# A batched matmul on one Trainium2 core: x loaded eight matrices at a time into single buffers

## The chip, the cores and the metric

The kernel runs on one core of one Trainium2 chip. The metric is the device time in microseconds, the median of several executions. "Span" is the time from the first to the last instruction in one profiled execution; it is some 1.5 to 1.8 us below the time. All runs that are compared here are of the fast state, but for three runs of a single execution, whose state is unknown; they are marked.

## The reference

```python
b1, b2, m, k, n = 8, 16, 256, 512, 384
x      = randn(b1, b2, m, k)   # float32
weight = randn(b1, b2, k, n)   # float32
return np.matmul(x, weight)    # float32
```

These are 128 products of 256x512 by 512x384. 167.8 MB are read, 50.3 MB are written.

## The kernel before

A round takes four matrices. Each partition gets 16 KB of x (eight rows), 12 KB of weights per pair of matrices, and gives back 12 KB of output. ScalarE casts x to bf16, and TensorE transposes pairs of bf16 as if they were fp32 words. VectorE copies the transposes out of PSUM and casts the weights, TensorE multiplies, ScalarE copies the result out, and SyncE issues all transfers on one queue. x has two landing buffers:

```python
XS, WS, OS = 2, 2 * G // D, 4        # landing slots of x, weights, output
BS, TS, WBS = 1, 2, 2 * G            # x in bf16, transposed x, weights in bf16
...
def load(e, t, U, s):
    n = t * U + s
    if not isinstance(n, int) or n >= XS:
        e.wait_ge(x_cast, n + (1 - XS))          # the cast of two rounds before
    e.dma_start(x_sb[s % XS][:], ...)            # 2 MB, runs of 16 KB
    for d in range(G // D):
        ...
        e.dma_start(w_sb[slot][:], ...)          # 1.5 MB
...
def step(t, U, s, more):                         # ScalarE
    for q in range(T):
        copy_out(e, t, U, s, q)
        if q == 1 and more:
            cast_x(e, t, U, s + 1)               # next round's x, amid the copies out
```

## Time and profile before

| | before |
|---|---|
| time, median | 519.8 us (519.78 to 519.87) |
| span | 518.3 us |
| transfers | 218.16 MB, 131 of them on one queue |
| busy share of PE, VectorE, ScalarE | 61%, 62%, 41% |

The page's slices cut the span in 40 equal parts; a digit is the busy share in tenths, and the row GB/s is what the sixteen DMA engines moved. The groups and the timeline give an instruction's line, its engine, what it writes and reads, and in brackets how long the engine was idle before it and what ended that. The lines are shown in the prediction below. The issuing engine's own waits, in total us, number and longest, show how tightly the queue was fed:

```profile
SPq L100 <- ACT x_bf L130: 257.1, 30, 9.4
SPq L108 <- DVE w_bf L148: 138.1, 58, 3.6
```

SyncE waits 257 us for x casts, yet a transfer takes a median of some 26 us from issue to landing. So these waits lie beside a long queue and cost nothing.

### The profile page before, as it was taken

To read this page: it belongs to the slowest core of one execution; us is meant where nothing else is said; L and a number is where in the kernel's file an instruction comes from. 1 tells how busy PE (TensorE), PEld (TensorE's weight loads), DVE (VectorE), ACT (ScalarE), POOL (GpSimd) and SP (SyncE) were. 2 spreads that over 40 slices of the span, in tenths; PEclk is the share of its full clock that TensorE was granted. 3 is DMA by queue.
4 is the path that set the end of the run, shared out by engine and by line. 5 is a ranking of instruction groups with operands and counts; after the bars stand their busy time and mean duration, and the time that the engine had idled before them with its cause. 6 is when DMAs were issued, how large, how long until landed. Compare 5 with 4: busy or idle time off the path is not lost.

```text
span 518.3 us, 11239 instructions
## 1 busy us (share of the span) xinstructions
PE 315.5 (61%) x4608; PEld 198.8 (38%) x4608; DVE 323.9 (62%) x384; ACT 212.7 (41%) x193; POOL 0.7 (0%) x6
## 2 busy tenths in 40 slices
PE   0686773576655675655756557665567665675653
PEld 0455452343433443433424334343344333443331
DVE  0878867655577555775556765557755577555670
ACT  3065462454234553245542445423454324553242
POOL 0000000000000000000000000000000000000000
PEclk9988788877687778678776877778787868886787
DMA  8999999999999999999999999999999999999995
GB/s 332 431 426 426 427 427 429 430 426 429 430 428 429 431 426 428 428 431 431 425 429 429 430 430 429 427 428 429 430 430 428 426 431 430 429 428 427 428 431 214
DMA packets 18868, 218.16 MB, mean 421 GB/s; under 512 B 2096, under 2 KB 2096, under 8 KB 2608
## 3 DMA queue, kind: packets, MB, share of 16 engines
q1 hardware_dynamic: 18864, 218.11, 99.2%
q8 instruction: 2, 0.03, 0.0%
q14 instruction: 2, 0.02, 0.0%
HBM read 167.77 MB, written 50.33 MB: 421 GB/s over the span
## 4 chain that ended last, share of the span: by engine, by line
DMA 81%; DVE 12%; issue 2%; PE 2%; ACT 1%; SPq 0%; DVEq 0%; ACTq 0%
DMA w_sb<-in_weight_dram 81%; DVE w_bf L148 12%; PE po L181 2%; ACT x_bf L130 0%; DVEq _compat.py:109 0%; SPq L108 0%; ACT out_sb L195 0%; SPq L100 0%; DVE x_t L154 0%; DVEq L143 0%; DVEq L230 0%; SPq L107 0%; ACTq L194 0%; SPq L288 0%; SPq L54 0%
## 5 line engine op out<-in xcount | busy, mean ns | idle before, releaser
L148 DVE CAST w_bf<-w_sb 64x1536 bf16<-64x1536 f32 x256 | 244.5, 955 | 179.4 <-DMA w_sb<-in_weight_dram 166.7
L181 PE MATMUL po<-w_bf,x_t 128*32 128x384 bf16 x4096 | 231.4, 400 | 121.0 <-DVE x_t L154 121.0
L195 ACT COPY out_sb<-po 128x768 f32<-128x768 f32 x128 | 99.2, 802 | 290.2 <-PE po L181 290.2
L181 PEld LDWEIGHTS po<-w_bf,x_t 128*32 128x32 bf16 x4096 | 124.5, 117 | 225.4 <-DVE x_t L154 130.9
L167 PE MATMUL pt<-identity,x_bf 128*128 128x128 f32 x512 | 84.0, 329 | 73.0 <-ACT x_bf L130 73.0
L130 ACT CAST x_bf<-x_sb 128x2048 bf16<-128x2048 f32 x64 | 118.4, 1901 | 6.1 <-DMA x_sb<-in_x_dram 6.1
L167 PEld LDWEIGHTS pt<-identity,x_bf 128*128 128x128 f32 x512 | 74.3, 213 | 84.9 <-issue 84.9
L154 DVE COPY x_t<-pt 128x1024 bf16<-128x1024 bf16 x128 | 79.5, 683 | 1.0
L130 ACT ACT_TABLE_LOAD x1 | 1.3, 1283 | 1.3 <-PEq L237 1.3
masks.py:199 POOL TENSOR_SCALAR_AFFINE_SELECT identity<-identity 128x128 f32<-128x128 f32 x1 | 0.3, 292 | 0.2 <-POOL identity L204 0.2
L204 POOL MEMSET identity<- 128x128 f32 x1 | 0.2, 204 | 0.5 <-SPq L54 0.5
L277 POOL MEMSET const-bfloat16-1.0<- 128x1 bf16 x1 | 0.1, 101 | 0.0
L277 POOL MEMSET const-uint8-127<- 128x1 uint8 x1 | 0.1, 101 | 0.0
L277 POOL MEMSET const-float32-0.0<- 128x1 f32 x1 | 0.1, 98 | 0.2 <-issue 0.2
L277 POOL MEMSET const-float32-1.0<- 128x1 f32 x1 | 0.1, 98 | 0.0
## 6 DMA issues: line engine op xcount, KB each, us to landing
w_sb<-in_weight_dram SPq DMA_DIRECT2D x64, 1536.0 KB, 27.5
x_sb<-in_x_dram SPq DMA_DIRECT2D x32, 2048.0 KB, 25.8
out_dram<-out_sb SPq DMA_DIRECT2D x31, 1536.0 KB, 30.6
out_dram<-out_sb SPq DMA_DIRECT2D x4, 384.0 KB, 3.6
```

The costliest lines, as they stand in the source:

```text
L130: ins = e.copy(out=x_bf[s % BS][:, :, h], in_=x_sb[s % XS][:].rearrange("p r (q s c) -> p r s q c", s=S, c=KO)[:, :, h],)
L148: e.tensor_copy(out=w_bf[(s * G + d * D + a) % WBS][h * HP : (h + 1) * HP], in_=w_sb[slot][a * HP : (a + 1) * HP, h * KO : (h + 1) * KO, : ...
L154: e.tensor_copy(out=x_t[s % TS][:, 2 * q : 2 * q + 2], in_=pt[(s * T + q) % PT][:].bitcast(bf16),).then_inc(t_copied, 1)
L167: ins = e.transpose(pt[(s * T + q) % PT][:, rr, h, :], words[:, 2 * q + rr, h :: KO // 2], identity[:],)
L181: ins = e.matmul(po[(s * T + q) % PO][mine, rr, :N], x_t[s % TS][:, 2 * q + rr, ko // 2, mine, ko % 2], w_bf[(s * G + i) % WBS][:, ko, :], ...
L195: e.copy(out=out_sb[s % OS][:, 2 * q : 2 * q + 2, :], in_=po[(s * T + q) % PO][:, :, :N],).then_inc(o_copied, 1)
L204: e.memset(identity[:], 0.0).then_inc(id_done, 1)
L277: nc = _bacc.Bacc("TRN2", target_bir_lowering=False, num_devices=1)
```

## The change

A group is now eight matrices. One x load brings 4 MB in runs of 32 KB into the only x buffer, and x_bf and x_t have one slot each as well. Transposes of the two halves of rows are written alternately into PSUM, word by word, so that 32 columns of x_t are one slice. Leaving out the drains on GpSimd is a side matter. The core of the diff:

```diff
-    XS, WS, OS = 2, 2 * G // D, 4
-    BS, TS, WBS = 1, 2, 2 * G
+    WS, OS, WBS = GX // D, 4, GX           # GX = 8
...
-    x_sb = sbuf("x_sb", [P, R, K], fp32, XS)
+    x_sb = sbuf("x_sb", [P, F * R, K], fp32)[0]      # F = 2
...
+    def load_x(e, n):
+        if not isinstance(n, int) or n > 0:
+            e.wait_ge(x_cast, n * (F * S))           # all four casts of the group before
+        e.dma_start(
+            x_sb[:], x_rows[bass.ds(n * (GX * M), GX * M)].rearrange("(p r) k -> p r k", p=P)
+        ).then_inc(x_in, 16)
...
                     ins = e.transpose(
-                        pt[(s * T + q) % PT][:, rr, h, :],
-                        words[:, 2 * q + rr, h :: KO // 2],
+                        pt[r % PT][:, h, :, f],
+                        words[:, f * R + r, h :: KO // 2],
...
     @block.scalar
-        cast_x(e, 0, NG, 0)
-        with e.Fori(0, NG // U - 1) as t:
-            for s in range(U):
-                step(t, U, s, True)
...
+        with e.Fori(0, NX // U) as t:
             for s in range(U):
-                step(t, U, s, True)
+                cast_x(e, t * U + s)
+                for f in range(F):
+                    copy_out(e, t * U + s, f, s * F + f, t)
```

More of the change, by code (lines that the diff above doesn't have):

```diff
@@ L39 @@
     G = 4
+    F = 2
+    GX = F * G
     C = P // G
@@ L45, with sbuf @@
     HP = P // D
-    NG = B // G
-    XS, WS, OS = 2, 2 * G // D, 4
-    BS, TS, WBS = 1, 2, 2 * G
+    NX = B // GX
+    WS, OS, WBS = GX // D, 4, GX
     PT, PO = 4, 2
     LAG = 4
-    ctx.enter_context(tc.tile_critical())
-    def sbuf(name, shape, dtype, n):
+    ctx.enter_context(tc.tile_critical(no_gpsimd_drain=True))
+    def sbuf(name, shape, dtype, n=1):
         return [
@@ L67, in sems @@
         return [tc.alloc_semaphore(f"{name}{s}") for s in range(n)]
-    identity = sbuf("identity", [P, P], fp32, 1)[0]
-    x_sb = sbuf("x_sb", [P, R, K], fp32, XS)
-    x_bf = sbuf("x_bf", [P, R, S, HP, KO], bf16, BS)
-    x_t = sbuf("x_t", [P, R, KO // 2, P, 2], bf16, TS)
+    identity = sbuf("identity", [P, P], fp32)[0]
+    x_sb = sbuf("x_sb", [P, F * R, K], fp32)[0]
+    x_bf = sbuf("x_bf", [P, F * R, S, HP, KO], bf16)[0]
+    x_t = sbuf("x_t", [P, R, KO // 2, P, F, 2], bf16)[0]
     w_sb = sbuf("w_sb", [P, S * KO, N], fp32, WS)
@@ L77 @@
     out_sb = sbuf("out_sb", [P, R, N], fp32, OS)
-    pt = psum("pt", [P, 2, KO // 2, P], fp32, PT)
+    pt = psum("pt", [P, KO // 2, P, F], fp32, PT)
     po = psum("po", [P, 2, 512], fp32, PO)
-    id_done, x_cast, w_cast, t_made, t_copied, p_made, o_copied = (
+    id_done, x_cast, w_cast, t_made, t_copied, p_made, o_copied, x_in = (
         sems(name, 1)[0]
         for name in (
-            "id_done", "x_cast", "w_cast", "t_made", "t_copied", "p_made", "o_copied"
+            "id_done", "x_cast", "w_cast", "t_made", "t_copied", "p_made", "o_copied",
+            "x_in",
@@ L88 @@
         )
     )
-    x_in, w_in, o_out = sems("x_in", XS), sems("w_in", WS), sems("o_out", OS)
+    w_in, o_out = sems("w_in", WS), sems("o_out", OS)
     BIAS = 8
-    def load(e, t, U, s):
-        n = t * U + s
-        if not isinstance(n, int) or n >= XS:
-            e.wait_ge(x_cast, n + (1 - XS))
+    def load_x(e, n):
+        if not isinstance(n, int) or n > 0:
+            e.wait_ge(x_cast, n * (F * S))
         e.dma_start(
-            x_sb[s % XS][:],
-            x_rows[bass.ds(n * (G * M), G * M)].rearrange("(p r) k -> p r k", r=R),
-        ).then_inc(x_in[s % XS], 16)
-        for d in range(G // D):
-            slot = (s * (G // D) + d) % WS
-            if not isinstance(n, int) or n >= 2:
-                e.wait_ge(w_cast, n * (G * S) + ((d + 1) * D * S - 2 * G * S))
+            x_sb[:], x_rows[bass.ds(n * (GX * M), GX * M)].rearrange("(p r) k -> p r k", p=P)
+        ).then_inc(x_in, 16)
@@ L108, in load, with load_w @@
+    def load_w(e, n, f):
+        for d in range(f * G // D, (f + 1) * G // D):
+            if not isinstance(n, int) or n > 0:
+                e.wait_ge(w_cast, n * (GX * S) + ((d + 1) * D * S - GX * S))
             e.dma_start(
-                w_sb[slot][:],
-                w_rows[bass.ds(n * (G * K) + d * (D * K), D * K)].rearrange(
-                    "(p k) n -> p k n", k=S * KO
-                ),
-            ).then_inc(w_in[slot], 16)
-    def store(e, t, U, s, pieces=1):
-        n = t * U + s
-        dram = o_rows[bass.ds(n * (G * M), G * M)].rearrange("(p r) n -> p r n", r=R)
+                w_sb[d][:],
+                w_rows[bass.ds(n * (GX * K) + d * (D * K), D * K)].rearrange(
+                    "(p k) n -> p k n", p=P
+                ),
+            ).then_inc(w_in[d], 16)
@@ L118, in store @@
+    def store(e, n, f, slot, pieces=1):
+        dram = o_rows[bass.ds(n * (GX * M) + f * (G * M), G * M)].rearrange(
+            "(p r) n -> p r n", p=P
+        )
         for q in range(pieces):
             rows = slice(q * R // pieces, (q + 1) * R // pieces)
-            e.wait_ge(o_copied, n * T + ((q + 1) * T // pieces + BIAS))
-            e.dma_start(out=dram[:, rows], in_=out_sb[s % OS][:, rows]).then_inc(
-                o_out[s % OS], 16
-            )
-    def cast_x(e, t, U, s):
-        n = t * U + s
-        e.wait_ge(x_in[s % XS], (t * (U // XS) + s // XS) * 16 + 16)
-        e.wait_ge(t_made, n * T + ((1 - BS) * T + BIAS))
-        for h in range(S):
-            ins = e.copy(
-                out=x_bf[s % BS][:, :, h],
-                in_=x_sb[s % XS][:].rearrange("p r (q s c) -> p r s q c", s=S, c=KO)[
-                    :, :, h
-                ],
-            )
-        ins.then_inc(x_cast, 1)
@@ L138, in prepare @@
-    def prepare(e, t, U, s):
-        n = t * U + s
-        e.wait_ge(p_made, n * T + (BIAS - T))
-        for d in range(G // D):
-            slot = (s * (G // D) + d) % WS
-            e.wait_ge(
-                w_in[slot], (t * (U * G // D // WS) + s * G // D // WS) * 16 + 16
-            )
-            for a in range(D):
-                for h in range(S):
-                    e.tensor_copy(
-                        out=w_bf[(s * G + d * D + a) % WBS][h * HP : (h + 1) * HP],
-                        in_=w_sb[slot][a * HP : (a + 1) * HP, h * KO : (h + 1) * KO, :],
-                    ).then_inc(w_cast, 1)
-        for q in range(T):
-            e.wait_ge(t_made, n * T + (q + 1 + BIAS))
-            e.tensor_copy(
-                out=x_t[s % TS][:, 2 * q : 2 * q + 2],
-                in_=pt[(s * T + q) % PT][:].bitcast(bf16),
-            ).then_inc(t_copied, 1)
@@ L159, in multiply @@
-    def multiply(e, t, U, s):
-        n = t * U + s
-        words = x_bf[s % BS][:].rearrange("p r s q c -> p r (s q c)").bitcast(fp32)
-        e.wait_ge(x_cast, n + 1)
-        for q in range(T):
-            e.wait_ge(t_copied, n * T + (q + 1 - PT + BIAS))
-            for rr in range(2):
+            e.wait_ge(o_copied, n * (F * T) + (f * T + (q + 1) * T // pieces + BIAS))
+            e.dma_start(out=dram[:, rows], in_=out_sb[slot][:, rows]).then_inc(
+                o_out[slot], 16
+            )
@@ new lines, in cast_x, with cast_w @@
+    def cast_x(e, n):
+        e.wait_ge(x_in, n * 16 + 16)
+        e.wait_ge(t_made, n * R + BIAS)
+        for f in range(F):
+            rows = slice(f * R, (f + 1) * R)
+            for s in range(S):
+                e.copy(
+                    out=x_bf[:, rows, s],
+                    in_=x_sb[:, rows].rearrange("p r (q s c) -> p r s q c", s=S, c=KO)[
+                        :, :, s
+                    ],
+                ).then_inc(x_cast, 1)
+    def cast_w(e, n, f):
+        e.wait_ge(p_made, n * (F * T) + (f * T + T - F * T + BIAS))
+        for d in range(f * G // D, (f + 1) * G // D):
+            e.wait_ge(w_in[d], n * 16 + 16)
+            for a in range(D):
+                for s in range(S):
+                    e.tensor_copy(
+                        out=w_bf[d * D + a][s * HP : (s + 1) * HP],
+                        in_=w_sb[d][a * HP : (a + 1) * HP, s * KO : (s + 1) * KO, :],
+                    ).then_inc(w_cast, 1)
@@ new lines, in copy_xt, with transpose @@
+    def copy_xt(e, n):
+        e.wait_ge(p_made, n * (F * T) + BIAS)
+        for r in range(R):
+            e.wait_ge(t_made, n * R + (r + 1 + BIAS))
+            e.tensor_copy(out=x_t[:, r], in_=pt[r % PT][:].bitcast(bf16)).then_inc(
+                t_copied, 1
+            )
+    def transpose(e, n):
+        words = x_bf[:].rearrange("p r s q c -> p r (s q c)").bitcast(fp32)
+        e.wait_ge(x_cast, n * (F * S) + F * S)
+        for r in range(R):
+            e.wait_ge(t_copied, n * R + (r + 1 - PT + BIAS))
+            for f in range(F):
@@ L172, in multiply @@
             ins.then_inc(t_made, 1)
-        e.wait_ge(w_cast, n * (G * S) + G * S)
+    def multiply(e, n, f):
+        e.wait_ge(w_cast, n * (GX * S) + (f + 1) * G * S)
         for q in range(T):
-            e.wait_ge(t_copied, n * T + (q + 1 + BIAS))
-            e.wait_ge(o_copied, n * T + (q + 1 - PO + BIAS))
+            if f == 0:
+                e.wait_ge(t_copied, n * R + (2 * q + 2 + BIAS))
+            e.wait_ge(o_copied, n * (F * T) + (f * T + q + 1 - PO + BIAS))
             for rr in range(2):
@@ L179, in multiply @@
                     for i in range(G):
-                        mine = slice(i * C, (i + 1) * C)
+                        lanes = slice((f * G + i) * (P // GX), (f * G + i + 1) * (P // GX))
                         ins = e.matmul(
-                            po[(s * T + q) % PO][mine, rr, :N],
-                            x_t[s % TS][:, 2 * q + rr, ko // 2, mine, ko % 2],
-                            w_bf[(s * G + i) % WBS][:, ko, :],
+                            po[q % PO][i * C : (i + 1) * C, rr, :N],
+                            x_t[:, 2 * q + rr, ko // 2, lanes, :, ko % 2].rearrange(
+                                "k p f -> k (p f)"
+                            ),
+                            w_bf[f * G + i][:, ko, :],
                             start=(ko == 0),
@@ L188, in multiply, with copy_out @@
             ins.then_inc(p_made, 1)
-    def copy_out(e, t, U, s, q):
-        n = t * U + s
-        if q == 0:
-            e.wait_ge(o_out[s % OS], (t * (U // OS) + s // OS) * 16 + 16)
-        e.wait_ge(p_made, n * T + (q + 1 + BIAS))
-        e.copy(
-            out=out_sb[s % OS][:, 2 * q : 2 * q + 2, :],
-            in_=po[(s * T + q) % PO][:, :, :N],
-        ).then_inc(o_copied, 1)
-    block = ctx.enter_context(nc.Block())
+    def copy_out(e, n, f, slot, turn):
+        e.wait_ge(o_out[slot], turn * 16 + 16)
+        for q in range(T):
+            e.wait_ge(p_made, n * (F * T) + (f * T + q + 1 + BIAS))
+            e.copy(
+                out=out_sb[slot][:, 2 * q : 2 * q + 2, :], in_=po[q % PO][:, :, :N]
+            ).then_inc(o_copied, 1)
+    block = ctx.enter_context(nc.Block(no_gpsimd_drain=True))
     @block.gpsimd
@@ L207, in _ @@
         e.drain().then_inc(id_done, 1)
+    U = OS // F
+    BACK = LAG // F
     @block.sync
     def _(e):
-        U = OS
-        for n in range(LAG):
-            load(e, 0, NG, n)
-        rounds = (NG - LAG) // U
+        for n in range(BACK):
+            load_x(e, n)
+            for f in range(F):
+                load_w(e, n, f)
+        rounds = (NX - BACK) // U
         with e.Fori(0, rounds) as t:
             for s in range(U):
-                load(e, t, U, LAG + s)
-                store(e, t, U, s)
-        for n in range(rounds * U, NG):
-            if n + LAG < NG:
-                load(e, 0, NG, n + LAG)
-            store(e, 0, NG, n, T if n == NG - 1 else 1)
+                load_x(e, t * U + (BACK + s))
+                for f in range(F):
+                    load_w(e, t * U + (BACK + s), f)
+                    store(e, t * U + s, f, (s * F + f) % OS)
+        for n in range(rounds * U, NX):
+            if n + BACK < NX:
+                load_x(e, n + BACK)
+            for f in range(F):
+                if n + BACK < NX:
+                    load_w(e, n + BACK, f)
+                last = n == NX - 1 and f == F - 1
+                store(e, n, f, (n * F + f) % OS, T if last else 1)
         for s in range(OS):
-            e.wait_ge(o_out[s], 16 + 16 * (NG // OS + (T - 1 if s == (NG - 1) % OS else 0)))
+            e.wait_ge(o_out[s], 16 + 16 * (NX // U + (T - 1 if s == OS - 1 else 0)))
     @block.vector
     def _(e):
-        U = 2
         e.sem_inc(t_copied, BIAS)
-        with e.Fori(0, NG // U) as t:
-            for s in range(U):
-                prepare(e, t, U, s)
+        with e.Fori(0, NX) as n:
+            cast_w(e, n, 0)
+            copy_xt(e, n)
+            for f in range(1, F):
+                cast_w(e, n, f)
     @block.tensor
     def _(e):
-        U = 2
         e.sem_inc(t_made, BIAS)
@@ L239, in _ @@
         e.wait_ge(id_done, 2)
-        with e.Fori(0, NG // U) as t:
-            for s in range(U):
-                multiply(e, t, U, s)
+        with e.Fori(0, NX) as n:
+            transpose(e, n)
+            for f in range(F):
+                multiply(e, n, f)
     @block.scalar
     def _(e):
-        U = OS
         e.sem_inc(o_copied, BIAS)
@@ L249, in _ @@
             e.sem_inc(o_out[s], 16)
-        def step(t, U, s, more):
-            for q in range(T):
-                copy_out(e, t, U, s, q)
-                if q == 1 and more:
-                    cast_x(e, t, U, s + 1)
-        cast_x(e, 0, NG, 0)
-        with e.Fori(0, NG // U - 1) as t:
+        with e.Fori(0, NX // U) as t:
             for s in range(U):
-                step(t, U, s, True)
-        for n in range(NG - U, NG):
-            step(0, NG, n, n < NG - 1)
+                cast_x(e, t * U + s)
+                for f in range(F):
+                    copy_out(e, t * U + s, f, s * F + f, t)
 _INS = ['x', 'weight']
```

## The prediction

> **What bounds the kernel now.** I read the page from the top: the slices, the chain that ended last and the queue, then the groups, and last the timeline of two inner rounds.
>
> ```profile
> span 518.3 us, 11239 instructions
> DMA  8999999999999999999999999999999999999995
> GB/s 332 431 426 426 427 427 429 430 426 429 430 428 429 431 426 428 428 431 431 425 429 429 430 430 429 427 428 429 430 430 428 426 431 430 429 428 427 428 431 214
> ...
> q1 hardware_dynamic: 18864, 218.11, 99.2%
> ...
> DMA 81%; DVE 12%; issue 2%; PE 2%; ACT 1%; SPq 0%; DVEq 0%; ACTq 0%
> ```
>
> The one DMA queue is never without work: every slice but the first and last is full, at 425 to 431 GB/s. The stretch from 20 to 490 us reads 429 GB/s. 218.16 MB at 428.6 GB/s are 509.0 us of the 518.3, so 9.3 us are head and tail. The chain is transfers for 81%; its 12% of VectorE is a cast between two transfers. No computing engine is near its limit:
>
> ```profile
> L148 DVE CAST w_bf<-w_sb 64x1536 bf16<-64x1536 f32 x256 | 244.5, 955 | 179.4 <-DMA w_sb<-in_weight_dram 166.7
> L181 PE MATMUL po<-w_bf,x_t 128*32 128x384 bf16 x4096 | 231.4, 400 | 121.0 <-DVE x_t L154 121.0
> L195 ACT COPY out_sb<-po 128x768 f32<-128x768 f32 x128 | 99.2, 802 | 290.2 <-PE po L181 290.2
> ...
> L167 PE MATMUL pt<-identity,x_bf 128*128 128x128 f32 x512 | 84.0, 329 | 73.0 <-ACT x_bf L130 73.0
> L130 ACT CAST x_bf<-x_sb 128x2048 bf16<-128x2048 f32 x64 | 118.4, 1901 | 6.1 <-DMA x_sb<-in_x_dram 6.1
> ...
> L154 DVE COPY x_t<-pt 128x1024 bf16<-128x1024 bf16 x128 | 79.5, 683 | 1.0
> ```
>
> VectorE waits 167 us for weights: it is fed by the queue, not the queue by it. A round of four matrices in the timeline, with the engine's idle time in brackets:
>
> ```profile
> 236.96 3.70 ACT L130 CAST x_bf<-x_sb 128x2048 bf16<-128x2048 f32 x2
> 238.33 7.86 DVE L148 CAST w_bf<-w_sb 64x1536 bf16<-64x1536 f32 x8 [5.68 <-DMA w_sb<-in_weight_dram]
> ...
> 240.79 2.18 PE L167 MATMUL pt<-identity,x_bf 128*128 128x128 f32 x16 [1.98 <-ACT x_bf L130]
> ...
> 246.22 2.48 DVE L154 COPY x_t<-pt 128x1024 bf16<-128x1024 bf16 x4
> ...
> 246.96 6.71 PE L181 MATMUL po<-w_bf,x_t 128*32 128x384 bf16 x128 [4.00 <-DVE x_t L154]
> ```
>
> The weight casts start every 15.93 us (222.27, 238.33, 254.25): a round's 2.10 MB of x, 3.15 of weights and 1.57 of output at 428.6 GB/s are 15.9 us. So the period is the transfers alone, and x for the next round is cast while this round still multiplies.
>
> **What the Trainium skill says.** (1) "DMA: Bandwidth & Descriptors", section "Where 436 GB/s comes from": sixteen ports give a ceiling of 435 GB/s. The trace agrees, at 428 to 429; at most 1.5% is left to win by any shape of transfer. (2) The same page, "Anatomy of one DMA": some 2.0 us of fixed cost, written of the GpSimd path. Here the first x load takes 7.8 us to land, of which 2.10 MB at 428.6 are 4.9, so 2.9 us; the last stores of 384 KB take 3.6, so 2.7. I use the measured 2.9. (3) "TensorE: Matmul & The Clock Gate", Part 1: PE idle for a window of about 3.4 us falls to half clock, and takes about as long to come back. The trace agrees: weight loads of four column tiles come every 0.32 us at the start of a round and faster later, and sixteen transposes take 2.18 us warm, 3.69 us at the first, cold ones. (4) "PSUM — Partial Sum Buffer", "Specifications (TRN2)": lines are of 8 bytes, and an access pattern that isn't contiguous slows matmuls. The kernel before writes its transposes contiguously, so its trace can't say.
>
> **The change part by part.** A group is now eight matrices, 16 groups. *Bytes* are the same: 13.63 MB a group, 31.8 us at 428.6. There are 16 x loads of 4 MB where there were 32 of 2 MB, with 128 runs of 32 KB each. Sixteen transfers fewer save 256 little completion writes out of 18,868 packets. If all that lies between 428.6 and 435 were a cost per run (1.5% of 16 KB at 27 GB/s an engine, some 9 ns; my estimate), halving 256 runs of x per engine would save 128 x 9 ns = 1.2 us. I count 0.5. *Compute* keeps every instruction count and shape: 512 transposes, 128 copies of 1,024, 64 x casts, 256 weight casts, 4096 matmuls. Only the transposes' outputs step by 8 bytes.
>
> *Buffers* are what changes. x_sb, x_bf and x_t have one slot each, and ScalarE does the four x casts of a group in one piece, only after all eight copies out of the group before. So the overlap of one group's x cast with the matmuls of the one before is gone, and a closed chain goes round once a group:
> - four x casts: 2 x 3.70 = 7.4 us;
> - handing over 0.13 (240.66 to 240.79 in the timeline);
> - 32 transposes on a PE that has idled 9 us: 16 cold 3.7, 16 warm 2.2, and the last copy to x_t 0.8: 6.7;
> - the second half of the weight casts, which VectorE's order puts behind the x_t copies: 8 x 0.98 = 7.9 (the first half's matmuls, 6 to 7 us, lie beside it);
> - 128 matmuls of the second half: 6.0 to 7.9 in the trace after various gaps; here a gap of 2 us comes before, 6.7;
> - the last copy out: 0.5 + 0.8 = 1.3, and two handings over 0.2.
>
> The sum is 30.3 us, against 31.8 us of transfers. The chain fits, with 1.5 us to spare where two rounds of the kernel before had about 10. What of it does the queue feel? The load of x(n+1) goes out as soon as the casts of x(n) end; until then the queue has the weights of n and the stores of n-2 before it, 9.4 MB or 22 us, and the casts take 7.6 us after landing. So in the steady state the load is asked for some 14 us early, and the queue doesn't run dry.
>
> *The head* has no such store of work. With 1.9 us from issue to first byte and 9.8 us for 4.19 MB, x(0) lands at 13.7 and is cast to 21.1; the weights of group 0 keep the queue busy to 27.3, x(1) to 37.1. VectorE casts half 0 from 17.3 to 25.2, copies x_t to 30.3, casts half 1 to 38.2. The matmuls end at 44.5, the copies out at 45.7. Only then are the casts of x(1), 45.7 to 53.1, and x(2) is issued at 53.2, with first bytes at 55.0. The weights of group 1 last to 51.8, and no store is yet queued before x(2), so the queue idles 3.2 us. A group later x(3) is asked for at 83.7, first bytes at 85.6, the queue ends at 86.8: no gap. From there the lead grows by 1.5 us a group.
>
> *The tail.* After the last x lands, the queue has 36.7 us of weights and stores; the last group's last output is ready 32 to 33 us after the landing (weights of the second slot cast by 11.5, x_t by 16.5, the weights left by 24.4, matmuls by 31, copy 32.2). The tail is then about as before: 3.7 us from the last bytes to the last completion and 1.6 to the end. The drains left out on GpSimd are 34 to 94 ns in the trace: 0.3 us at most.
>
> Sum: 2.9 start + 508.5 transfers + 3.2 idle in the head + 0.5 in the tail + 3.7 + 1.6 - 0.3 = 520.1 of span. The kernel before is timed 1.5 us above its span (519.78 to 518.3), so **521.5 us**.
>
> **The rivals.** (a) *The chain becomes the bound.* If the interleaved PSUM writes cost what the skill's PSUM page warns of, or PE stays cold, each of its terms grows: 32 cold transposes are 7.4 instead of 5.9, cold matmuls 7.9 instead of 6.7, together +2.7, and the period would be 33.0. Then x(3) and all after it come late, 1.2 us a group over 13 groups: some 16 us more, 537. For it: no slack of size, one slot each. Against it: a transposed column takes 1 ns even warm, slow enough for single words, and the matmuls were seen at 6.0 after a short gap. (b) *Nothing is seen*: the head's idle time is smaller (the cast of half 1 or the cold transposes shorter) and the time stays at 519. (c) *Longer runs are worth more than I count*: at the full 435 GB/s for all of x (67 MB) 2.3 us would be won, 519. A rate higher than the ceiling isn't to be had, so over 2% faster (under 509.4, less than the transfers and the start now take) is nearly shut out.
>
> **Range and chances.** Around 521.5, the head's idle time may be off by 2 us and the tail by 3; the low end, 516, takes gains in both and in the runs. The upper side is longer for rival (a), whose step is T - 31.8 times 13: T of 32.5 gives 530. I put (a) at over 530 at 0.12, faster at 0.03, and 0.85 within 2%.
>
> **What would show it.** Right: slices of the queue full but for one dip of some 3 us near 52 to 55; the rate 428 to 430; ScalarE's x casts in pieces of 7.4 us after which PE idles 8 to 9 us; the wait of the x issue for ScalarE's casts once above the queue's lead and then below it; transposes at about the same mean. Wrong: slices of 8 or 7 all the way with a period of the casts above 31.9 us (rival a), the mean of a transpose well over 329 ns (PSUM steps), a rate above 431 (long runs), or a tail in which the last matmuls come long after the last load.

## The result, and the profile after

The changed kernel takes **526.13 us** (525.51 to 526.91, 4 runs) against 519.81 for the kernel before in the same rounds. The ratio is 1.0122 (95% interval 1.0105 to 1.0140). The change is 1.2% slower: within 2%, and within the range, but 4.6 us above the predicted centre.

The page of the changed kernel, its span, slices and groups:

```profile
span 523.7 us, 11048 instructions
DMA  8999999999999999999999999999999999999993
GB/s 344 432 428 398 377 403 440 413 427 434 417 437 422 443 418 430 445 415 439 421 423 436 426 444 416 435 426 428 445 415 436 425 427 441 418 445 415 432 412 137
...
L169 PE MATMUL pt<-identity,x_bf 128*128 128x128 f32 x512 | 100.9, 380 | 162.7 <-ACT x_bf L136 159.0
...
L136 ACT CAST x_bf<-x_sb 128x2048 bf16<-128x2048 f32 x64 | 116.7, 1896 | 0.1
...
L136 ACT ACT_TABLE_LOAD x8 | 10.3, 1283 | 17.8 <-DMA x_sb<-in_x_dram 17.7
```

The row of busy digits looks full, but the row GB/s has three weak slices, 398, 377 and 403, near 39 to 79 us. The last slice holds 137 instead of 214. PE now idles 159 us for the x casts where it idled 73, as expected of the closed chain. And there are eight table loads of ScalarE where there was one: the new loop has no activation ahead of it, so the load stands in the loop's body (in hoist, below, it is one again).

The waits of the issuing engine, and the head of the timeline (start, duration, then as in the groups):

```profile
SPq L104 <- ACT x_bf L136: 220.7, 15, 18.4
SPq L112 <- DVE w_bf L149: 189.4, 37, 8.8
```

```profile
37.55 6.65 PE L186 MATMUL po<-w_bf,x_t 128*32 128x384 bf16 x128 [4.20 <-DVE w_bf L149]
...
44.95 7.30 ACT L136 CAST x_bf<-x_sb 128x2048 bf16<-128x2048 f32 x4
...
52.38 6.16 PE L169 MATMUL pt<-identity,x_bf 128*128 128x128 f32 x32 [8.18 <-ACT x_bf L136]
52.47 0.35 SPq L104 DMA_DIRECT2D x_sb<-in_x_dram  x1
```

The casts of the second group's x begin only after the first group is copied out, at 44.95, and the third x load is issued at 52.47. By then the queue has run dry. The windows of before and after show it (columns: stretch, its length, busy time of PE, weight loads, VectorE, ScalarE, GpSimd, the granted clock, the DMA engines' busy share and GB/s). First the kernel before, then the changed one:

```profile
50.00:53.00 3.00, 2.37 (x60) 1.33 (x52) 2.24 (x3) 3.00 (x3) 0.00 (x0) 1.00 1.03 436
53.00:56.00 3.00, 1.65 (x10) 1.66 (x11) 2.91 (x4) 2.62 (x3) 0.00 (x0) 0.86 1.02 434
70.00:74.00 4.00, 3.60 (x62) 2.24 (x64) 3.24 (x5) 0.61 (x1) 0.00 (x0) 0.72 1.01 428
```

```profile
50.00:53.00 3.00, 0.62 (x3) 0.63 (x4) 0.57 (x1) 2.25 (x2) 0.00 (x0) 0.50 0.54 229
53.00:56.00 3.00, 3.00 (x16) 3.00 (x15) 2.08 (x3) 0.00 (x0) 0.00 (x0) 0.50 1.06 350
70.00:74.00 4.00, 4.00 (x92) 2.40 (x88) 3.32 (x5) 2.34 (x3) 0.00 (x0) 0.89 0.98 347
```

Against 428.6 GB/s the first two windows lack 3 x 200 + 3 x 79 = 837 KB, or 2.0 us. The third lacks 4 x 82 = 326 KB, or 0.8 us, with the engines counted as busy: its packets took longer, next to the first stores. (A window counts the packets that start in it, so with runs of 32 KB a short one can read above the rate that the queue holds, as 489 below does.)

That is 2.8 of the 5.4 us of span. Where is the rest? Every transfer leaves sixteen records of completion, one for each DMA engine. I read these from both traces. The table gives the lag, how long the last engine's record comes after the median of the sixteen, for the transfer that lands nearest to a given time (us):

```text
landing near     100   200   300   400   500
before           1.9   1.9   2.7   3.2   3.7
after            0.5   1.7   2.6   4.3   5.7
```

For the last store that isn't cut into pieces the median record is at 508.5 us before and 510.8 after, the last record at 513.0 and at 518.2. The last 24 packets of data in both traces are 3 KB each and start one behind the other, some 0.12 us apart. So in both kernels **one engine arrives long after the others and ends the program**. Of the 5.2 us between the last records, 2.3 are in the median (the gap, less what longer runs save), and 2.9 are this engine's greater lag. The longer packets are cheaper as foreseen: 1213 ns (median) for 32 KB against 2 x 611 = 1222.

Where does the lag begin? The traces show that too. In both kernels two packets of 16 KB are instruction fetches (the page's queue q8): at 28.4 and 37.9 us before, at 33.3 and 42.6 after, of 1.06 to 1.11 us each. In the changed kernel the last engine's lag goes from 0.2 to 1.6 us at the first of them, the second-last engine's from 0.2 to 1.6 at the second; before, from 0.4 to 1.7 and from 0.4 to 1.4. The gap at the head then takes the lag back to 0.2 in the changed kernel, and at 143.8 us, after a few store packets of up to 2367 ns, it is 1.8 again. Why those were slow isn't known.

From 246 us on, the lag of the changed kernel jumps at most groups' second store. The packets of this store that take over 480 ns, when 460 is the rule, are these near 440 us (start, ns):

```text
437.10 489   437.58 521   438.10 540   438.64 521
439.16 526   439.68 521   440.20 521   440.71 521
```

Each starts when the one before it ends, so they belong to one engine. The median engine had landed that store at 436.5. The last engine is still storing when the others have gone on to the next x load, and these eight packets take 0.48 us more than at 460 ns; its lag grows by 0.45 there. In the kernel before, no packet of 12 KB takes 515 ns or more between 220 and 490 us.

### The profile page after: what moved, and what is told of

Same layout as the page of the kernel before. It is cut to its first block, busy times and chain, and to the rows that moved or that the text cites. A ratio compares the mean times of both kernels' runs of the same rounds, so it can differ in the third digit from the quotient of the medians.

```text
span 523.7 us, 11048 instructions
## 1 busy us (share of the span) xinstructions
PE 293.5 (56%) x4608; PEld 207.8 (40%) x4608; DVE 325.8 (62%) x384; ACT 228.6 (44%) x200; POOL 0.7 (0%) x6
## 4 chain that ended last, share of the span: by engine, by line
DMA 39%; ACT 20%; PE 18%; DVE 12%; issue 8%; DVEq 1%; SPq 1%; ACTq 0%
DMA x_sb<-in_x_dram 29%; ACT x_bf L136 18%; PE po L186 12%; DVE w_bf L149 10%; PE pt L169 7%; DMA w_sb<-in_weight_dram 5%; DMA out_dram<-out_sb 4%; DVE x_t L158 2%; ACT L136 2%; DVEq _compat.py:109 0%; SPq L104 0%; ACT out_sb L201 0%; SPq L112 0%; DVEq L245 0%; ACTq L132 0%
## 5 line engine op out<-in xcount | busy, mean ns | idle before, releaser
L186 PE MATMUL po<-w_bf,x_t 128*32 128x384 bf16 x4096 | 193.8, 353 | 58.6 <-DVE w_bf L149 58.6
L201 ACT COPY out_sb<-po 128x768 f32<-128x768 f32 x128 | 102.4, 800 | 269.2 <-PE po L186 269.2
L169 PE MATMUL pt<-identity,x_bf 128*128 128x128 f32 x512 | 100.9, 380 | 162.7 <-ACT x_bf L136 159.0
L186 PEld LDWEIGHTS po<-w_bf,x_t 128*32 128x32 bf16 x4096 | 113.3, 104 | 135.5 <-DVE w_bf L149 64.8
L169 PEld LDWEIGHTS pt<-identity,x_bf 128*128 128x128 f32 x512 | 94.5, 220 | 171.2 <-issue 164.7
L136 ACT CAST x_bf<-x_sb 128x2048 bf16<-128x2048 f32 x64 | 116.7, 1896 | 0.1
L158 DVE COPY x_t<-pt 128x1024 bf16<-128x1024 bf16 x128 | 81.4, 685 | 32.7 <-PE pt L169 32.3
```

What stands on the lines that cost most here:

```text
L136: e.copy(out=x_bf[:, rows, s], in_=x_sb[:, rows].rearrange("p r (q s c) -> p r s q c", s=S, c=KO)[:, :, s],).then_inc(x_cast, 1)
L158: e.tensor_copy(out=x_t[:, r], in_=pt[r % PT][:].bitcast(bf16)).then_inc(t_copied, 1)
L169: ins = e.transpose(pt[r % PT][:, h, :, f], words[:, f * R + r, h :: KO // 2], identity[:],)
L186: ins = e.matmul(po[q % PO][i * C : (i + 1) * C, rr, :N], x_t[:, 2 * q + rr, ko // 2, lanes, :, ko % 2].rearrange("k p f -> k (p f)"), w_b ...
L201: e.copy(out=out_sb[slot][:, 2 * q : 2 * q + 2, :], in_=po[q % PO][:, :, :N]).then_inc(o_copied, 1)
```

## The experiments

The theories: **A**, the gap at the head; **B**, the shape of the x transfers; **C**, the computing chain as the bound; later **D**, the last engine's stores slowed where an x load follows, and **E**, that the lag is only what instruction fetches put on one engine, and chance.

| run | time, median us | ratio to before (95%) | lag at 500 us |
|---|---|---|---|
| changed kernel | 526.13 | 1.0122 (1.0105 to 1.0140) | 5.7 |
| hoist | 527.25 | 1.0140 (1.0123 to 1.0157) | 7.0 |
| order | 525.23 | 1.0099 (1.0082 to 1.0116) | 9.3 |
| runs16 | 528.70 | 1.0169 (1.0152 to 1.0186) | 6.6 |
| half | 523.46 | 1.0062 (1.0046 to 1.0079) | 6.1 |
| smove | 524.95 | 1.0098 (1.0079 to 1.0117) | 3.3 |
| order_smove | 519.48 | 0.9990 (0.9973 to 1.0007) | 3.0 |
| tail | 519.36 | 0.9989 (0.9975 to 1.0002) | 4.2 |

All of these gave correct results. Runs that were sent together ran on one chip: the first four after the changed kernel, then smove, order_smove and the two queue kernels, then tail with queue32_lag, then the two seeded kernels. The intervals of hoist, order and smove overlap that of the changed kernel, so differences of about 1 us from it are at the edge of what these rounds can tell; half, runs16, order_smove and tail are clear of it. The lags are of one profiled execution each.

### hoist: one table load

```diff
-        with e.Fori(0, NX // U) as t:
-            for s in range(U):
-                cast_x(e, t * U + s)
-                for f in range(F):
-                    copy_out(e, t * U + s, f, s * F + f, t)
+        cast_x(e, 0)
+        with e.Fori(0, NX // U - 1) as t:   # in it: copy_out of both halves, then cast_x of the next
```

> The changed kernel with the x casts of the next group written at the end of the loop body, and the first ones ahead of the loop, so that ScalarE's table load (1.28 us) happens once at the start and no longer in each pass. Theory A (the loss is a gap in the queue at the head: x of group 2 is asked for only after group 0 is copied out and x of group 1 is cast): the table load before the first cast is gone, the third x load is issued at 51.2 instead of 52.5 us, the queue's gap falls from 2.0 to 0.7 us, and the time falls by 1.3, to 524.8. Theory B (the loss is the shape of the transfers: one DMA engine falls behind the others faster, 5.7 us behind the median at 500 us where the kernel before has 3.7): nothing changes, 526. Theory C (the computing chain sets the pace): eight table loads fewer are 10 us less, 516.

It took 527.25 us, no faster. The table load is gone from the loop, and the first casts begin at 13.15 instead of 14.53. But the third x load went out at 52.66, not 51.2. Group 0 waits for VectorE's weight casts: the first half of them runs from 16.8 to 24.7 in both kernels, ahead of the x_t copies, so an earlier x is worth nothing there. Theory C falls: seven loads fewer (one is left), 9.0 us of ScalarE, won nothing. My figure for A rested on a wrong path through group 0; the gap itself was the same, 233 GB/s in the window from 50 to 53. Why hoist came out 1.1 us above the changed kernel isn't settled; its profiled execution has the larger lag.

### order: x casts between the two halves

```diff
             for f in range(F):
                 copy_out(e, n, f, s * F + f, turn)
-                if f == 1 and more:         # hoist
+                if f == 0 and more:         # order
                     cast_x(e, n + 1)
```

> As hoist, but ScalarE casts the next group's x between the copies out of the two halves, beside the wait for weights, instead of after both. Theory A: the third x load is issued some 8 us earlier, the queue has no gap at the head, the time falls by 2 to 2.5 us against the changed kernel, to about 523.8. Theory B: 526. Theory C: the chain loses 7.4 us a group and the time falls to the queue's, 519 to 520.

525.23 us: 2.0 below hoist and 0.9 below the changed kernel. The third x load is issued at 46.74, and the window from 50 to 53 moves 489 GB/s instead of 229. So the gap is gone, and yet little is won. In place of it the lag reaches 9.3 us at 500. At 100 us it is 2.1, where the changed kernel has 0.5: the gap had let the last engine catch up. The lag costs more than the end of one engine: every cast waits for all sixteen, and between the last two whole stores the median records lie 7.3 us apart (503.4 and 510.7), where the one before came after 3.6.

### runs16 and half: smaller loads, then smaller waits

runs16:

```diff
-        e.dma_start(x_sb[:], dram).then_inc(x_in, 16)
+        for f in range(F):
+            rows = slice(f * R, (f + 1) * R)
+            e.dma_start(x_sb[:, rows], dram[:, rows]).then_inc(x_in, 16)
```

> The changed kernel with each 4 MB x load issued as two of 2 MB with 16 KB runs, one right after the other, both waiting for all four casts as before. Theory A: the gap stays, 526. Theory B: with 16 KB runs the slowest engine's lag at 500 us returns to about 3.7 us, the time falls by 2 to 3 us, to 523.5; a packet of 16 KB takes 611 ns against 1213 for 32 KB, so 1.2 us of that is given back.

528.70 us: a miss of both theories. The lag is as large as with long runs (6.6), so run length isn't its cause. The 2.6 us that it lost have a visible part at the head. The matmuls of group 0's second half happened to take 7.87 us instead of 6.65, on a slower clock, and the third x load went out at 53.73. Twice as many x packets cost 1.2 us, by their durations.

half adds a wait for each half's own two casts (and the casts of a half wait only for its own load):

```diff
         for f in range(F):
             rows = slice(f * R, (f + 1) * R)
+            if not isinstance(n, int) or n > 0:
+                e.wait_ge(x_cast, n * (F * S) + ((f + 1) * S - F * S))
-            e.dma_start(x_sb[:, rows], dram[:, rows]).then_inc(x_in, 16)
+            e.dma_start(x_sb[:, rows], dram[:, rows]).then_inc(x_in[f], 16)
```

> As runs16, but each half of x has its own semaphore and waits only for its own two casts, so the first half is asked for 3.65 us earlier. Theory A: the third x load is issued at 48.8 us, before the queue runs dry at about 52, no gap is left, and the time is 2 to 2.5 us below that of runs16. Theory B: the same as runs16. Theory C: the casts of a landed half can start sooner, but the chain itself is unchanged, so the same as the changed kernel.

523.46 us, 5.2 below runs16 and 2.7 below the changed kernel, though its x packets are the short ones. The two windows of half where the changed kernel had its gap:

```profile
50.00:53.00 3.00, 0.00 (x0) 0.00 (x0) 0.69 (x1) 3.00 (x2) 0.00 (x0) 0.50 1.02 434
53.00:56.00 3.00, 2.83 (x13) 2.84 (x14) 1.38 (x2) 0.03 (x1) 0.00 (x0) 0.50 1.01 430
```

The queue is full where it was empty, 434 and 430 for 229 and 350. Two kernels that differ only in these waits differ by 5.2 us, so the gap is a real cost; runs16's gap was the longer one (250 and 98 GB/s in these windows).

### smove and order_smove: no store right before an x load

```diff
                 for f in range(F):
-                    load_w(e, t * U + (BACK + s), f)
+                    load_w(e, t * U + (BACK + s), f, (0,))
                     store(e, t * U + s, f, (s * F + f) % OS)
+                    load_w(e, t * U + (BACK + s), f, (1,))
```

> The changed kernel with each store issued before the last weight load of its half instead of after it, so that no store stands right before an x load in the queue. In the changed kernel's trace, and in hoist, order, runs16 and half, the packets of 12 KB that take 520 to 550 ns instead of 460 stand one behind the other at the end of each group's second store, where only the engine that is last is still storing and the others have begun the next x load. Theory D (the last engine's stores are slowed beside the others' x loads, so its lag grows by itself): those packets go, the lag of the last engine behind the median at 500 us falls from 5.7 to 2 to 3 us, and the time from 526 to 523; the gap at 53 us stays. Theory E (the lag is only what the instruction fetches put on one engine, and chance): the lag and the time stay, 526.

524.95 us (523.9 to 525.95), 1.2 below the changed kernel. Between 220 and 490 us only three packets of 12 KB are left that take 515 ns or more, where the changed kernel had 47. The lag at 500 us is 3.3 instead of 5.7. So the place of the stores feeds the lag, as D has it. That it is the x load as such that slows them isn't shown: in the kernel before, every store stands right before an x load too, without such packets; and the edit also puts a weight load behind each store. The time fell by less than the 3 us that I gave it, too: the gap stands, and here it cost more, since the third x load went out at 53.16 and the window from 53 to 56 moved 179 GB/s. Packets of 515 ns or more in the same stretch number 48 in hoist, 45 in order, 42 in runs16, 27 in half, and none in order_smove.

> order (x casts between the copies out of the two halves) and smove together: the gap at the head and the stores before x loads are both taken away. Theory D: the lag at 500 us falls from the 9.3 us of order to 2 to 3 us, the time from 525.2 to 519 to 520, as the kernel before; the halved number of x packets saves 1.2 us of that per engine. Theory E: as order, 525.

519.48 us, as D had it. The gap is gone, the lag stays flat (2.6, 2.5, 2.6, 2.7, 3.0), and the last x lands at 476.8 us instead of 483.5. The whole loss of the changed kernel is back: 6.65 us, where order alone gave 0.9 and smove alone 1.2. From order to order_smove only the place of the stores changes, and that is 5.75 us; from smove to order_smove only the place of the x casts, and that is 5.5. The lag that is left, 2.6 us from 66 us on, was there before any of the late growth, and part of it came with the instruction fetches (1.7 at 45 us): so much of E is true. The two parts don't add up, it seems, because each alone leaves the other to set the end: without the gap the last engine starts behind and falls behind further, and without the growing lag the gap stays. The stretch from 20 to 490 us in order_smove:

```profile
20.00:490.00 470.00, 291.01 (x4321) 183.16 (x4322) 305.44 (x365) 202.28 (x181) 0.00 (x0) 0.81 1.01 430
```

It moves 430 GB/s, against 426 in the changed kernel and 429 in the kernel before.

### tail: the last weights before the stores

```diff
+            if n + BACK == NX - 1:
+                for f in range(F):
+                    load_w(e, n + BACK, f)          # all of the last group's weights, then the stores
```

> order_smove, with the loads of the last group all issued before the stores of the group two before, since no x load follows them. In order_smove most engines idle some 4 us near 509 to 513, where the last group's outputs are not yet there: its last weights stood behind two stores, 7.3 us. If the idle engines are what is lost, these come earlier and the time falls from 519.5 by 3 to 4 us, to 516; if the engine that is last has no idle time to lose there (its lag in order_smove is some 2.6 us), it falls by 1 to 2 us, to 518. Either would beat the kernel before, 519.9.

519.36 us, the same as order_smove to 0.1 us; the interval for the ratio to the kernel before, 0.9975 to 1.0002, just includes 1. The last engine's lag was 4.2 us at 500 in the profiled execution, and its records of the last three whole stores come 3.8 and 4.1 us apart, so it had nothing idle to win back. So moving work for the other fifteen gave nothing, and neither this kernel nor order_smove beats the one before by an amount that these rounds can tell.

### The queue alone

Two kernels issue only the transfers, with no waits for computing, and write zeros. They begin 13 us late (first issue at 13.92 instead of 0.96), since four output buffers are cleared first. Their outputs are wrong, which doesn't matter for the times.

```diff
-            e.wait_ge(x_cast, n * (F * S))
+            e.wait_ge(x_in, n * 16)         # only: the load before has landed
```

> Only the transfers of the changed kernel, in its order, none waiting for any computation (each load waits for the one before it in the same buffer, stores wait for nothing; the output is zero and wrong on purpose). Theory B or D (the shape or the order of the transfers): packets of 520 to 550 ns appear at the second store of each group, the lag grows as in the changed kernel, and the span is some 2 to 3 us over queue16's; there is no gap at the head. Theory A alone: 2 us below the changed kernel's head, no growing lag, span 517 to 518.

> Only the transfers of the kernel before in its order: x in 2 MB pieces that are contiguous in memory with 16 KB runs, otherwise as queue32. Theory B: no slow packets, the lag at 500 us near 3 us, span 516 to 518, 2 to 3 us below queue32. Theory D with the x load as the slower: the same as queue32, since here too each store stands before an x load. Theory A: 1.2 us above queue32, as its x packets number twice as many.

queue32, with the changed kernel's transfers in its order, took 529.74 us, and queue16, with those of the kernel before, took 531.04. Less the 12.96 us of late start, 516.8 and 518.1. The two differ by 1.3 us, near the 1.2 worked out from the packets. But in the profiled executions only 0.8 us lies between the median records of the last whole store; the rest is lag, which in queue16 was the larger (0.5, 1.8, 2.6, 2.7, 2.9 at the five times). So the larger x transfers are worth about 1 us, and the close agreement is in part chance. The kernel before stands 1.7 us above its bare queue, the changed one 9.3. Neither the gap nor a steady growth of the lag is in queue32 (0.2, 0.4, 0.4, 1.9, 1.8 at the five times), though each group's second store stands before an x load there too. So B falls. Packets of 515 ns or more do occur in queue32, 19 of them between 220 and 490 us, and one in queue16; but they lie scattered, of 519 to 1253 ns, not one behind the other at the end of a store. D as I had put it, from the transfers alone, isn't shown by queue32; but there was hardly an engine behind for it to act on: these kernels have no fetch on q8, and their lag is at most 0.7 us at 100 us.

> Placeholder run withdrawn if refused: the transfers of the changed kernel alone once more, a second look at the growth of the lag without any lag made on purpose: the lag stays under 2 us at 500 us and the span is near 527.9.

It is of one execution: 529.94 us, lag 1.9 at 500. The two seeded kernels add, at the fourth group:

```diff
+            if n == 3:
+                e.dma_start(pad[0:47, 0:K], x_rows[0:47, :]).then_inc(pad_in, 16)
```

> queue32 with one more transfer at the fourth group (47 rows of 2 KB, which all go through one DMA engine), so that this engine falls some 4 us behind the others, with no computation anywhere. Theory D from transfers alone: from there on the second store of each group shows packets of 520 to 550 ns, as in the changed kernel, and the lag of the last engine grows from 4 to 7 us or more by 500 us. If the computation is needed for it: the lag stays near 4 us to the end.

> The same extra transfer in queue16, the order and shape of the kernel before. If the 4 MB x loads are what slows the last engine's stores: the lag stays near 4 us or grows by the 1 to 2 us that it grew in the kernel before and in queue16. If any x load behind a store does it: it grows as in queue32_seed.

Both are single executions: 531.87 and 533.09 us, 2.1 and 2.0 above the medians of the unseeded kernels, for 94 KB more. The lag of the last engine rises at this transfer from 0.3 to 4.0 us in queue32_seed, while the second-last's is 0.4. At the five times:

```text
landing near     100   200   300   400   500
queue32_seed     0.3   3.8   4.0   3.8   3.8
queue16_seed     0.6   3.9   3.9   3.8   3.7
```

It stays where it was put. So a late engine beside an x load isn't enough: in these two executions the growth didn't come without the whole kernel, its computation or its timing. And one engine held up by a small transfer moves the end of the whole program.

## Why the prediction was right or wrong

- **The bound and the chain: right.** The transfers bound both kernels. The chain was put at 30.3 us a group. Two groups' casts start at 44.95 and 106.32 us, 30.7 each, of which half of a 1.28 us table load is 0.6; without it, 30.05. Rival (a), the chain as the bound, didn't come: hoist took ScalarE work off the chain and won nothing.
- **The head: right in mechanism and place, a bit large.** The gap was forecast at 51.8 to 55.0 us, 3.2 us long, from a third x load issued at 53.2. It was issued at 52.47, and the two windows lack 2.0 us. With the slower packets at 70 to 74, which I had not foreseen, the head lost 2.8. order and half take the gap away.
- **The runs of 32 KB: right.** 9 ns for each run of 16 KB saved was the estimate; 1222 - 1213 = 9 ns for each pair was measured, 1.2 us in all, and about 1 us for the queue alone. I had counted only 0.5 of it.
- **The transposes' 8-byte steps: no cost seen.** Their mean rose from 329 to 380 ns, which I had named as the sign of such a cost. But sixteen cold transposes (at half the granted clock) take 3.68 us as before (3.69), and 32 warm ones take 4.10 in order, where 16 took 2.18 in the kernel before. More of them are cold, that is all.
- **The tail and the sum: this step failed.** The sum took the sixteen engines as one queue ("508.5 transfers", "0.5 in the tail"). Both kernels end with one engine that is behind: 4.5 us at the last stores before, 7.4 after. The 2.9 us between them are most of the 3.6 by which the span missed (523.7 for 520.1). The term "3.7 us from the last bytes to the last completion" had read this engine's late stores as a delay of completion: in the kernel before, the last packet of data ends at 516.28 and the last record comes at 516.68. The sum was short from the start: without the change it gives 2.9 + 509.0 + 3.7 + 1.6 = 517.2 for a span of 518.3. The range held by luck: it allowed the tail 3 us, but not for this reason, and its upper side was drawn for rival (a), which didn't come. smove shows that the place of the stores in the queue feeds this lag; order_smove, that the lag and the gap together are the whole loss. *Why* the last engine's stores slow down from 460 to 520 ns there, and neither in the kernel before nor one after another in the queue alone, isn't settled.
- **The table loads** in the loop were missed in reading the diff. They cost nothing measurable (hoist).

## What to carry to other kernels

A single buffer that is refilled only after a chain of computing is harmless while a long queue stands before the refill; look at the first rounds, where no queue has built up. Where the queue is the bound, read its completions engine by engine: the mean busy share can be full while one engine of sixteen decides the end, and then a gap, the order of stores and loads, and that engine's lag don't simply add up. A change that lengthens runs and one that drops a buffer are best tried apart: here the longer runs were worth about 1 us, and the changed kernel as a whole lost 6.3. The single buffers need not cost it: order_smove has them too, with another order of casts and stores, and takes the time of the kernel before.

## What the Trainium skill lacked or had wrong

- "DMA: Bandwidth & Descriptors" says in passing that a bulk load runs at the pace of its slowest engine. It lacks that over some 130 queued transfers one engine can fall behind and stay behind, and so set the end: 3.7 us behind the median at 500 us before, 9.3 us in order, and a seeded 3.8 us that stayed flat for 300 us and cost 2 us of time.
- The same page lacks that store packets of such an engine can slow down, 460 to 520 and 550 ns for 12 KB, as they did at the end of the store that stands before an x load in the changed kernel and four of its variants (27 to 48 packets between 220 and 490 us). In order_smove, with the stores moved, there were none; in the kernel before, whose stores stand before x loads too, there were none either, so the cause is open.
- "PSUM — Partial Sum Buffer" says that any non-contiguous pattern slows matmuls. For fp32 transposes of 128 columns written at a step of 8 bytes no run here shows it: 3.68 us for sixteen cold ones against 3.69 contiguous.
